# Hyena's transforms over odd frequencies, split into even and odd tokens, inside a two-layer mixer network

## The chip, the cores and the metric

The kernel runs on one core of one Trainium2 chip. The metric is device time in microseconds (us) of the whole network: the median of three runs before the change is 2637.45 us, from 2637.12 to 2638.57. A difference of about 0.2%, here 5 us, is the least that a comparison of two such kernels can tell from no change.

Engines have the names of the profile: PE is TensorE, PEld its weight loads, DVE is VectorE, ACT is ScalarE, POOL is GpSimd, and SP (SPq in rows) is the engine that issues the DMAs here.

## The reference, cut to what matters

Two layers work on 256 latent tokens and 256 context tokens of width 1024. A layer is a SwiGLU FFN, four token mixers on one normalised input (MLA, gated linear attention "GLA", GQA, and Hyena), merged by gates, and a second FFN. In the second layer the context's mixer output isn't needed. The change touches Hyena alone:

```python
def hyena_filters(L, w1, b1, w2, b2, w3):
    ...
    h = h * jnp.exp(-t[:, None] * deltas[None, :])[:, None, None, :]
    full = jnp.concatenate([h[:, :, 0], jnp.zeros(...), jnp.flip(h[1:, :, 1], axis=0)], axis=0)
    return jnp.fft.rfft(full.astype(jnp.float32), axis=0)

def fft_long_conv(u, filt_f, bias):
    L = u.shape[1]
    U = jnp.fft.rfft(u.astype(jnp.float32), n=2 * L, axis=1)
    y = jnp.fft.irfft(U * filt_f[None], n=2 * L, axis=1)[:, :L]
    return (y + u * bias).astype(u.dtype)

def hyena_mixer(p, hy):
    z = lax.conv_general_dilated(p, sconv_w[:, None, :], ...) + sconv_b
    x1, x2, v = jnp.split(z, 3, axis=-1)
    filt = hyena_filters(p.shape[1], w1, b1, w2, b2, w3)
    v = x1 * fft_long_conv(v, filt[:, 0], fbias[0])
    v = x2 * fft_long_conv(v, filt[:, 1], fbias[1])
    return v
```

Each of the 512 channels of a sequence of L = 256 tokens is convolved with a filter that reaches 255 tokens to both sides, then multiplied by a gate, twice ("orders", `od` 0 and 1 in the code).

## The kernel before

**Matmuls.** Every large product is done as three matmuls of the type fp32r: each operand is held as a rounded part ("h", a CAST on ACT) and a rest ("l", a subtraction on DVE), and `mm3` (L305) adds h·h, h·l and l·h into PSUM. `two` (L311) makes such a pair: `nc.scalar.copy` for h and `nc.vector.tensor_sub` for l. Weights come from DRAM by DMAs on SP into three buffers `wr` and are split in the same way into `wh` and `wl` (eight buffers each), 512 columns at a time, on ACT and DVE. While `self.share` is set, which is in the second layer's Hyena and GLA stage alone, the rest `wl` is made on POOL instead.

**Transforms as matmuls.** `tables` (L100) holds three matrices of 256 tokens by 256 frequencies (`dft`: cosines, negative sines, and the sines of the way back, with the Nyquist frequency in a row of their own). `dft(n)` (L1084) loads n of them and splits each into a pair.

**Filters.** `filters` (L1105) makes the spectra of both layers' filters once, in the first FFN, where its steps are fillers between the FFN's rows. For each layer and order it makes the filter in time (`h3`, tiles `hx`), forms sum and difference of its two directions on POOL (L1155, L1156), splits them (`hy`), and multiplies by the tables: for two halves m of the frequencies and for real and imaginary part e, six matmuls `sp` of 512 channels. Four more matmuls `nyq` with one column of weights give the Nyquist row. The spectra go to DRAM (`hs`, five tiles for each layer and order) from SBUF tiles `spx` and `spn` of the pool `t`, which has six buffers.

**Hyena.** `hyena` (L1189) runs for both sequences in the first layer (`nseq` = 2) and for the latent one in the second (`nseq` = 1). It projects and convolves over three tokens (`conv`, PSUM tile `dp`). For each order it transposes the current value to tokens (eight 128x128 transposes `zT` a sequence), splits it (`zth`, `ztl`), and for each sequence does 24 matmuls `Z` of 512 channels (two halves m, real and imaginary part), the complex product with the spectrum on DVE (L1241 to L1246), the split into `Y`, and 48 matmuls `yi` of 256 tokens, which have the channels as weights' columns, so that the result has channels on the partitions again. The gate `gx` is multiplied there (L1260, L1263).

**Order of the work.** A scheduler of the programming layer sets the order on each engine when the program is built, from priorities and from its own picture of when results are ready; each engine then works strictly in that order. `weave` (L1302) alternates between "chains", which have a raised priority, and a "fill". In the first layer the chain is `hyena`, the fill is `prep` (all other projections, PSUM tile `tm`). In the second layer the chains are `hyena` and `gla`, the fill is two `merge`s (PSUM tile `gate`). In `gla` (L951) the matmuls `AT` need the decayed keys `ab` (L1017), and the transposes `obT` the normalised output `z` (L1073), both from DVE. PSUM has two buffers each for the tags `S` (which `Z`, `sp`, `ada` and others use) and `T` (`zT`, `yi` and others).

Of the kernel before, what the change touches and what calls it, by code (L numbers as in the profile page):

```python
# [44 lines left out]
for _n, _w in (("kcos", 64), ("ksin", 64), ("spec", 2)):  # L45
    TAB[_n] = (_o, _w)
    _o += _w
# [18 lines left out]
          "end2": {"p": 11, "y": 4, "Yh": 4, "Yl": 4, "lv": 6, "lg": 4}}  # L66
SHARE = {"first": {"x": "v"},
         "ffn": {"x": "v"},
         "mix": {k: v for v, ks in (("v", "x hv mv lv"), ("p", "hp hH mp qp lp yh"), ("g", "hg mg qg lg yl"),
# [30 lines left out]
def tables():  # L100
# [17 lines left out]
    sp = np.full((P, 2), 2.0 / 512, np.float32)  # L118
    sp[0, 0] = 1.0 / 512
    put("spec", sp)  # L120
# [4 lines left out]
    T["ident"] = np.eye(P, dtype=np.float32)  # L125
    t = np.arange(L)
    ang = 2 * np.pi * ((t[:, None] * t[None, :]) % 512) / 512
    fre, fim = np.cos(ang), -np.sin(ang)
    ifim = fim.copy()
    fim[:, 0] = ifim[0, :] = (-1.0) ** t  # L130
    T["dft"] = np.stack([m.reshape(2, P, L).transpose(1, 0, 2) for m in (fre, fim, ifim)], 0).reshape(3, P, 512)
# [4 lines left out]
    T["feat"] = np.concatenate([tl[:, None], np.cos(fw), -np.sin(fw)], -1).T  # L136
    dl = np.abs(np.linspace(math.log(1e-2) / 1.5, math.log(1e-2) / 0.3, 512, dtype=np.float32))
    wf = np.exp(-tl[:, None] * dl[None, :]).astype(np.float32)
# [83 lines left out]
class Net:  # L222
# [150 lines left out]
    def load(self):  # L373
# [24 lines left out]
        self.hs = self.dram.tile([DEPTH, 2, 5, P, 512], F32, name="hs")  # L398
# [706 lines left out]
    def filters(self):  # L1105
# [25 lines left out]
        F = self.dft(2)  # L1131
# [4 lines left out]
        for l in range(DEPTH):  # L1136
            for od in range(2):
# [26 lines left out]
                sp = self.tab["spec"]  # L1164
                for m in range(2):
                    for e in range(2):
                        p = self.pss("sp")
                        for k in range(2):
                            c = slice(k * L + m * P, k * L + m * P + P)
                            self.mm3(p, (F[e][0][:, c], F[e][1][:, c]), ab[k][e], k == 0, k == 1)  # L1170
                        x = self.t("spx")
                        nc.scalar.activation(x, p, AF.Copy, scale=sp[:, m:m + 1])
                        if m == 0 and e == 1:
                            nc.gpsimd.memset(x[0:1], 0.0)
                        nc.sync.dma_start(out=self.hs[l, od, 2 * m + e], in_=x)
                        if m == 0 and e == 0:
                            pn = self.pst("nyq")
                            for k in range(2):
                                c = slice(k * L, k * L + 1)
                                for i, z in enumerate(ab[k][0]):  # L1180

                                    self.mm(pn[:1], F[1][0][:, c], z, k == 0 and i == 0, k == 1 and i == 1)
# [226 lines left out]
```

## Time and profile before

| | before |
|---|---|
| median of three runs | 2637.45 us |
| profiled execution | 2630.62 us |
| its span (first to last instruction) | 2628.8 us |
| mean granted TensorE clock | 0.989 |
| PE busy | 2536.3 us, 96% |
| DVE busy | 1663.5 us, 63% |
| ACT busy | 1088.0 us, 41% |
| POOL busy | 241.7 us, 9% |

The profile is of one execution. Its 2628.8 us of span lie in 2630.62 us of device time; the median of the runs without a profile is 6.83 us above that. A PE row's length runs from the start of a matmul to its modelled end and overlaps the next one, so the pace of a row of matmuls is read from start to start. The same goes for DVE, whose instructions overlap by some 0.08 us. Three stretches matter: about 60 to 225 us, where the filters are made within the first FFN; 475 to 700 us, the first layer's Hyena; and 2125 to 2325 us, the second layer's Hyena and GLA.

### The profile page before, as it was taken

To read this page: it belongs to the slowest core of one execution; us is meant where nothing else is said; L and a number is where in the kernel's file an instruction comes from. 1 tells how busy PE (TensorE), PEld (TensorE's weight loads), DVE (VectorE), ACT (ScalarE), POOL (GpSimd) and SP (SyncE) were. 2 spreads that over 40 slices of the span, in tenths; PEclk is the share of its full clock that TensorE was granted. 3 is DMA by queue.
4 is the path that set the end of the run, shared out by engine and by line. 5 is a ranking of instruction groups with operands and counts; after the bars stand their busy time and mean duration, and the time that the engine had idled before them with its cause. 6 is when DMAs were issued, how large, how long until landed. Compare 5 with 4: busy or idle time off the path is not lost. (4 is left out here: it accounts for less than half of the span.)

```text
span 2628.8 us, 37485 instructions
## 1 busy us (share of the span) xinstructions
PE 2536.3 (96%) x13952; PEld 2098.2 (80%) x13952; DVE 1663.5 (63%) x3326; ACT 1088.0 (41%) x2114; POOL 241.7 (9%) x232
## 2 busy tenths in 40 slices
PE   6999999999999999999999999999999988899998
PEld 4667888799976767786888878888888777798998
DVE  5556677655555868746744447767457666776665
ACT  4332323423455464433323233232345655355454
POOL 2120001200000000001000021000030045401000
PEclk9999999999999999999999999999999999899999
DMA  7436455433322323336543244545254334356554
GB/s 255 155 133 232 137 184 178 151 116 105 106 87 92 94 63 97 96 104 211 175 143 96 93 137 150 182 143 181 85 176 161 104 124 150 97 170 213 175 181 126
DMA packets 123901, 371.93 MB, mean 141 GB/s; under 512 B 14210, under 2 KB 19780, under 8 KB 123720
## 3 DMA queue, kind: packets, MB, share of 16 engines
q1 hardware_dynamic: 123720, 369.55, 43.5%
q8 instruction: 110, 1.80, 0.3%
q14 instruction: 71, 0.58, 0.1%
HBM read 348.00 MB, written 21.50 MB: 141 GB/s over the span
## 5 line engine op out<-in xcount | busy, mean ns | idle before, releaser
L313 ACT CAST wh<-wr 128x512 fp32r<-128x512 f32 (+1 forms) x926 | 564.2, 613 | 1090.7 <-PE gu L303 395.5
L314 DVE TENSOR_TENSOR wl<-wr,wh 128x512 fp32r<-128x512 f32 (+1 forms) x854 | 578.2, 683 | 449.9 <-ACT wh L313 439.0
L303 PE MATMUL gu<-ul,wh 128*128 128x512 f32 (+1 forms) x1408 | 514.2, 366 | 2.8 <-DVE ul L544 2.7
L303 PE MATMUL gu<-uh,wh 128*128 128x512 f32 (+1 forms) x1408 | 511.8, 365 | 2.5 <-ACT uh L538 2.3
L303 PE MATMUL gu<-uh,wl 128*128 128x512 f32 (+1 forms) x1408 | 511.1, 364 | 1.3 <-DVE wl L314 1.3
L303 PE MATMUL dn<-hh,wh 128*128 128x512 f32 (+1 forms) x1408 | 391.8, 365 | 0.0
L303 PEld LDWEIGHTS gu<-ul,wh 128*128 128x128 f32 x1408 | 266.2, 189 | 58.4 <-DVE ul L544 8.0
L303 PEld LDWEIGHTS gu<-uh,wh 128*128 128x128 f32 x1408 | 266.6, 190 | 51.2 <-ACT uh L538 7.0
L303 PEld LDWEIGHTS gu<-uh,wl 128*128 128x128 f32 x1408 | 266.2, 189 | 43.8 <-issue 2.0
L303 PEld LDWEIGHTS dn<-hh,wh 128*128 128x128 f32 x1408 | 255.1, 190 | 41.7
L303 PE MATMUL dn<-hh,wl 128*128 128x512 f32 (+1 forms) x704 | 256.8, 365 | 0.0
L504 POOL TENSOR_TENSOR nacc<-nacc,sq 128x512 f32<-128x512 f32 (+1 forms) x39 | 46.0, 1178 | 1773.0 <-ACT sq L502 1765.6
L303 PE MATMUL gate<-uh,wh 128*128 128x256 f32 (+1 forms) x768 | 200.9, 326 | 0.0
L466 DVE SCALAR_TENSOR_TENSOR aj<-aw,crow 128x1024 bf16<-128x1024 f32 x160 | 194.0, 1225 | 3.0 <-DMA crow<-cb 3.0
L303 PE MATMUL gate<-uh,wl 128*128 128x512 f32 (+1 forms) x512 | 176.0, 344 | 0.3 <-POOL wl L314 0.3
L303 PEld LDWEIGHTS dn<-hh,wl 128*128 128x128 f32 x704 | 133.9, 190 | 20.8
L303 PE MATMUL tm<-wh,uh 128*128 128x256 f32 x576 | 140.0, 288 | 1.6 <-ACT uh L538 1.0
L303 PEld LDWEIGHTS gate<-uh,wh 128*128 128x128 f32 x768 | 130.7, 194 | 11.6 <-issue 2.3
L303 PE MATMUL tm<-wl,uh 128*128 128x256 f32 x432 | 124.0, 287 | 0.0
L314 POOL TENSOR_TENSOR wl<-wr,wh 128x512 fp32r<-128x512 f32 x72 | 100.8, 1412 | 245.4 <-ACT wh L313 225.7
L303 PE MATMUL tm<-wh,ul 128*128 128x256 f32 x416 | 107.8, 286 | 0.0
L303 PEld LDWEIGHTS gate<-uh,wl 128*128 128x128 f32 x512 | 98.7, 193 | 11.2 <-issue 1.7
(390 smaller groups left out, 4023.1 us busy)
## 6 DMA issues: line engine op xcount, KB each, us to landing
wr<-in_gu SPq DMA_DIRECT2D x176, 512.0 KB, 3.5
aw<-in_adat SPq DMA_DIRECT2D x80, 512.0 KB, 3.6
wr<-in_dn SPq DMA_DIRECT2D x64, 512.0 KB, 3.8
wr<-in_w_gate SPq DMA_DIRECT2D x64, 512.0 KB, 3.5
aw<-in_ada SPq DMA_DIRECT2D x48, 512.0 KB, 5.3
wr<-in_w_tm SPq DMA_DIRECT2D x36, 512.0 KB, 3.5
wr<-in_w_br SPq DMA_DIRECT2D x32, 512.0 KB, 3.5
wr<-in_dn SPq DMA_DIRECT2D x32, 384.0 KB, 3.2
```

Of the source, the lines that this page charges most:

```text
L303: self.nc.tensor.matmul(out, l, r, start=start, stop=stop)
L313: self.nc.scalar.copy(h, src)
L314: (eng or self.nc.vector).tensor_sub(l, src, h)
L466: nc.vector.scalar_tensor_tensor(out=x, in0=w, scalar=1.0, in1=self.crow[s], op0=ALU.mult, op1=ALU.mult, accum_out=o[:, s:s + 1])
L504: (nc.vector if first and k % 2 else nc.gpsimd).tensor_add(acc[:, :n], acc[:, :n], sq[:, :n])
```

## The change

The transforms are taken at odd frequencies, at the angles 2π(2f+1)t/1024, f from 0 to 255, instead of 2πft/512. Frequency 255 − f has, but for signs, the same values as f: with the tokens split by parity, the even tokens' sum and the odd tokens' sum of the first 128 frequencies give f as their sum and 255 − f as their difference. So one table of 128 points, in four blocks of 128x128 (cosine and negative sine, even and odd tokens), serves in place of three of 256 by 256, and one more holds the blocks transposed for the way back. There is no Nyquist row.

- `half` (new) does one block: three matmuls of 512 channels, or six where it adds a second block.
- In `filters` each part e takes two halves (12 matmuls `sp` for a layer and order in place of 24, and no `nyq`), and DVE makes sum and difference of them from PSUM (two instructions for each e), ACT a scaled copy. Four stores in place of six.
- In `hyena` a sequence of one order takes 12 matmuls `Z`; ACT copies one half, DVE makes sum and difference (`za`, `zb`); the complex products are ten DVE instructions and two on POOL; four more on DVE combine f with 255 − f before the way back; four pairs `Yh`, `Yl`; 12 matmuls `yi` of 512 channels whose weights are the table's blocks. The result has tokens on the partitions, all even or all odd ones.
- So for order 0 the gates are transposed to tokens (`yT`, eight transposes of every second token) and multiplied there, and the product is split at once for order 1 (`nz`), which needs no transpose of its own. For order 1 the result is copied by ACT, transposed back (eight `yT`), and multiplied by every second token of the gate, in eight DVE instructions of 128x128.
- Four spectrum tiles `H` are loaded in place of five, two tables in place of three. In the second layer's stage the pools are eight in place of eleven `p`, three in place of four `Yl`, and four new `za`.

```diff
-          "end2": {"p": 11, "y": 4, "Yh": 4, "Yl": 4, "lv": 6, "lg": 4}}
+          "end2": {"p": 8, "y": 4, "za": 4, "Yh": 4, "Yl": 3, "lv": 6, "lg": 4}}
...
-         "mix": {k: v for v, ks in (("v", "x hv mv lv"), ("p", "hp hH mp qp lp yh"), ("g", "hg mg qg lg yl"),
+         "mix": {k: v for v, ks in (("v", "x hv mv lv"), ("p", "hp hH mp qp lp yh"), ("g", "hg za mg qg lg yl"),
...
     t = np.arange(L)
-    ang = 2 * np.pi * ((t[:, None] * t[None, :]) % 512) / 512
-    fre, fim = np.cos(ang), -np.sin(ang)
-    ifim = fim.copy()
-    fim[:, 0] = ifim[0, :] = (-1.0) ** t
-    T["dft"] = np.stack([m.reshape(2, P, L).transpose(1, 0, 2) for m in (fre, fim, ifim)], 0).reshape(3, P, 512)
+    ang = 2 * np.pi * ((t[:, None] * (2 * np.arange(P)[None, :] + 1)) % 1024) / 1024
+    fwd = [f(ang[e::2]) * g for f, g in ((np.cos, 1.0), (np.sin, -1.0)) for e in range(2)]
+    T["dft"] = np.stack([np.concatenate(fwd, 1), np.concatenate([m.T for m in fwd], 1)])
+    par = np.concatenate([t[0::2], t[1::2]])
...
-        self.hs = self.dram.tile([DEPTH, 2, 5, P, 512], F32, name="hs")
+        self.hs = self.dram.tile([DEPTH, 2, 4, P, 512], F32, name="hs")
...
-        F = self.dft(2)
+        F = self.dft(1)[0]
...
-                sp = self.tab["spec"]
-                for m in range(2):
...
-                            nc.sync.dma_start(out=self.hs[l, od, 4, 0:1], in_=xn[0:1])
+                for e in range(2):
+                    p = [self.half(F, 2 * e + k, ab[k][e], "sp") for k in range(2)]
+                    x, y, z = (self.t("spx") for _ in range(3))
+                    nc.scalar.activation(x, p[0], AF.Copy, scale=2.0 / 512)
+                    nc.vector.scalar_tensor_tensor(out=y, in0=p[1], scalar=2.0 / 512, in1=x, op0=ALU.mult, op1=ALU.add)
+                    nc.vector.scalar_tensor_tensor(out=z, in0=p[1], scalar=(2 * e - 1) * 2.0 / 512, in1=x,
+                                                   op0=ALU.mult, op1=ALU.subtract if e else ALU.add)
+                    nc.sync.dma_start(out=self.hs[l, od, 2 * e], in_=y)
+                    nc.sync.dma_start(out=self.hs[l, od, 2 * e + 1], in_=z)
                 yield
+    def half(self, F, q, x, name, y=None, r=0):
+        p = self.pss(name)
+        for q, x, last in ((q, x, y is None), (r, y, True)):
+            if x is not None:
+                c = slice(q * P, q * P + P)
+                self.mm3(p, (F[0][:, c], F[1][:, c]), x, y is None or not last, last)
+        return p
     def hyena(self, l, u, nseq, out):
         nc, A = self.nc, self.A
@@ -1206,64 +1199,95 @@
         for i in range(4):
             conv(8 + i, src[i])
             yield
-        F = self.dft(3)
+        F, G = self.dft(2)
+        def parity(x, s, e):
+            return x[:, s * L + e:s * L + L:2]
+        zt = []
+        for i in range(2 * nseq):
+            T = self.pst("zT")
+            for c in range(4):
+                self.tr(T[:, c * P:c * P + P], parity(src[c], i // 2, i % 2))
+            h, lo = self.tl("o", "zth", 512, F32R), self.tl("o", "ztl", 512, F32R)
+            self.two(h, lo, T)
+            zt.append((h, lo))
+        yield
         for od in range(2):
-            zt = []
-            for t in range(2 * nseq):
...
-            H = [self.ld(self.tl("hH", "H"), self.hs[l, od, i]) for i in range(5)]
+            H = [self.ld(self.tl("hH", "H"), self.hs[l, od, i]) for i in range(4)]
             gx = self.packed("hg" if od else "hv", "hx", n, 4)
             for i in range(4):
                 conv(4 * od + i, gx[i])
                 if i % 2:
                     yield
-            if od == 0:
-                dst = self.packed("hv", "z1", n, 4)
-            else:
+            if od:
                 dst = [self.pair("o", "od", n) for _ in range(4)]
+            nz = []
             for s in range(nseq):
+                z = []
+                for e in range(2):
+                    p = [self.half(F, 2 * e + k, zt[2 * s + k], "Z") for k in range(2)]
+                    x, y = self.tl("za", "za"), self.tl("za", "zb")
+                    nc.scalar.copy(y, p[0])
+                    nc.vector.tensor_add(x, y, p[1])
+                    if e:
+                        nc.vector.tensor_sub(y, p[1], y)
+                    else:
+                        nc.vector.tensor_sub(y, y, p[1])
+                    z += [x, y]
+                yield
+                a, b, c, d = z
+                q = []
+                for x, y, hx, hy in ((a, c, H[0], H[2]), (b, d, H[1], H[3])):
+                    v, w = self.t("yv"), self.t("yw")
+                    nc.gpsimd.tensor_mul(v, y, hy)
+                    nc.vector.tensor_mul(w, x, hx)
+                    nc.vector.tensor_mul(x, x, hy)
+                    nc.vector.tensor_mul(y, y, hx)
+                    nc.vector.tensor_sub(w, w, v)
+                    nc.vector.tensor_add(x, x, y)
+                    q.append(w)
+                nc.vector.tensor_sub(d, a, b)
+                nc.vector.tensor_add(a, a, b)
+                nc.vector.tensor_add(c, q[0], q[1])
+                nc.vector.tensor_sub(b, q[0], q[1])
                 Y = []
-                for m in range(2):
-                    pz = []
...
-                        self.mm3(p[:, :L], (Y[q][0][:, cc], Y[q][1][:, cc]), (f[0][:, fc], f[1][:, fc]), q == 0, q == 3)
+                for x in (c, d, b, a):
+                    Y.append((self.tl("Yh", "Yh", 512, F32R), self.tl("Yl", "Yl", 512, F32R)))
+                    self.two(*Y[-1], x)
+                yield
+                T = []
+                for e in range(2):
+                    p = self.half(G, e, Y[2 * e], "yi", Y[2 * e + 1], 2 + e)
+                    T.append(self.pst("yT"))
+                    x = self.t("yx")
+                    for c in range(4):
+                        if od == 0:
+                            self.tr(T[e][:, c * P:c * P + P], parity(gx[c], s, e))
                     if od == 0:
-                        nc.vector.tensor_mul(dst[c][:, cs], p[:, :L], gx[c][:, cs])
+                        nc.scalar.copy(x, T[e])
+                        nc.vector.tensor_mul(x, p, x)
+                        h, lo = self.tl("o", "zth", 512, F32R), self.tl("o", "ztl", 512, F32R)
+                        self.two(h, lo, x)
+                        nz.append((h, lo))
                     else:
-                        x = self.t("od")
-                        nc.vector.tensor_mul(x[:, :L], p[:, :L], gx[c][:, cs])
-                        self.two(dst[c][0][:, cs], dst[c][1][:, cs], x[:, :L])
+                        nc.scalar.copy(x, p)
+                        for c in range(4):
+                            self.tr(T[e][:, c * P:c * P + P], x[:, c * P:c * P + P])
+                if od:
+                    cs = slice(s * L, s * L + L)
+                    for c in range(4):
+                        if c % 2 == 0:
+                            x = self.t("od")
+                        xc = x[:, c % 2 * L:c % 2 * L + L]
+                        for e in range(2):
+                            nc.vector.tensor_mul(xc[:, e::2], T[e][:, c * P:c * P + P], parity(gx[c], s, e))
+                        self.two(dst[c][0][:, cs], dst[c][1][:, cs], xc)
                 yield
-            src = dst
+            zt = nz
         out.extend(dst)
```

PE, first layer, first sequence of order 0. `Z` are the transforms, `tm` the fill's projections, `yi` the way back. Before (the line of dots stands for the tm rows up to 37 in all):

```order
L303 MATMUL Z<-ztl,dfth 128x512
L303 MATMUL tm<-wl,uh 128x256
L303 MATMUL Z<-zth,dftl 128x512
L303 MATMUL tm<-wh,ul 128x256
...
L303 MATMUL tm<-wh,ul 128x256
L303 MATMUL yi<-dfth,Y 128x256
L303 MATMUL tm<-wh,uh 128x256
L303 MATMUL yi<-dftl,Y 128x256
```

Now (the dots stand for the tm rows up to 84 in all):

```order
L301 MATMUL Z<-zth,dfth 128x512
L301 MATMUL Z<-ztl,dfth 128x512
L301 MATMUL Z<-zth,dftl 128x512
L301 MATMUL tm<-wh,ul 128x256
...
L301 MATMUL tm<-wl,uh 128x256
L301 MATMUL yi<-Yh,dfth 128x512
L301 MATMUL tm<-wh,ul 128x256
L348 MATMUL yT<-ident,hx 128x128
```

The scheduler puts 84 matmuls of the fill between the last `Z` and the first `yi` where it put 37. At the first layer's three other places of this kind there are now 82 `tm`, 73 `tm`, and 21 `tm` with 24 `bk` of 512 columns. The transposes `yT` stand one by one between other matmuls. In the second layer more than 200 `gate` and `dp` rows, and GLA's, stand between the last `Z` and the first `yi` of each order.

DVE at the same place, from the first use of the last `Z` on. `wl` is the fill's weights. Before:

```order
L1243 TENSOR_TENSOR yb<-Z,H 128x512
L1244 TENSOR_TENSOR yd<-Z,H 128x512
L1245 TENSOR_TENSOR ya<-ya,yb 128x512
L1246 TENSOR_TENSOR yc<-yc,yd 128x512
L314 TENSOR_TENSOR Y<-ya,Y 128x512
L314 TENSOR_TENSOR Y<-yc,Y 128x512
```

Now (the dots stand for a copy `vr` of the fill, the sum of `za`, and for `zb` the same five products and sums):

```order
L1234 TENSOR_TENSOR za<-zb,Z 128x512
L1236 TENSOR_TENSOR zb<-Z,zb 128x512
L1246 TENSOR_TENSOR yw<-za,H 128x512
L1248 TENSOR_TENSOR za<-za,H 128x512
L1247 TENSOR_TENSOR za<-za,H 128x512
L1249 TENSOR_TENSOR yw<-yw,yv 128x512
...
L1255 TENSOR_TENSOR za<-yw 128x512
L1253 TENSOR_TENSOR zb<-za,zb 128x512
L312 TENSOR_TENSOR wl<-wr,wh 128x512
L1254 TENSOR_TENSOR za<-za,zb 128x512
L312 TENSOR_TENSOR Yl<-za,Yh 128x512
```

Three instructions led from there to the value that is split first (L1245), on values of both parts; now there are fourteen with the copy, up to the row L1255, after which ACT makes the first `Yh`.

SP, the stores of the third spectrum. Before:

```order
L322 DMA wr<-in_dn 128x1024 x5
L1175 DMA hs<-spx 128x512
L1183 DMA hs<-spx 127x512
L1186 DMA hs<-spn 1x512
L1175 DMA hs<-spx 128x512 x2
L291 DMA fb<-in_hfb 1x512
L1175 DMA hs<-spx 128x512
```

Now:

```order
L320 DMA wr<-in_dn 128x1024 x5
L1169 DMA hs<-spx 128x512
L1170 DMA hs<-spx 128x512
L289 DMA fb<-in_hfb 1x512
L1169 DMA hs<-spx 128x512
L1170 DMA hs<-spx 128x512
```

The store of one row, `hs<-spn`, is gone, and with it the store of the other 127.

## Rows read from the trace of the kernel before

**Rows 1.** The page: busy us, share of the span, and instructions of each engine.
```profile
PE 2536.3 (96%) x13952; PEld 2098.2 (80%) x13952; DVE 1663.5 (63%) x3326; ACT 1088.0 (41%) x2114; POOL 241.7 (9%) x232
```

**Rows 2.** Windows: length, then busy us (instructions) of PE, PEld, DVE, ACT, POOL.
```profile
475.00:700.00 225.00, 224.07 (x1414) 200.53 (x1411) 128.12 (x219) 78.87 (x147) 10.17 (x17) 1.00 0.34 114
2125.00:2325.00 200.00, 173.01 (x1263) 158.26 (x1262) 147.49 (x286) 99.82 (x194) 90.57 (x65) 0.95 0.40 127
60.00:225.00 165.00, 152.00 (x646) 115.15 (x645) 84.97 (x137) 58.90 (x99) 25.26 (x20) 0.96 0.50 170
```

**Rows 3.** Timeline of PE, filters: start, length, instruction.
```profile
191.85 1.09 PE L303 MATMUL nyq<-hy,dfth 128*1 128x512 f32 x4
192.78 0.62 PE L303 MATMUL sp<-hy,dfth 128*128 128x512 f32 x2
...
196.89 0.61 PE L303 MATMUL dn<-hh,wh 128*128 128x512 f32 x2
```

**Rows 4.** Timeline of PE, second layer's last way back.
```profile
2314.20 0.53 PE L303 MATMUL yi<-dfth,Y 128*128 128x256 f32 x3
2314.56 0.28 PE L303 MATMUL yi<-dftl,Y 128*128 128x256 f32 x1
```

**Rows 5.** Timeline of PE, transposes among other matmuls.
```profile
502.48 0.82 PE L350 MATMUL zT<-ident,hv 128*128 128x128 f32 x6
503.06 0.36 PE L303 MATMUL tm<-wh,ul 128*128 128x256 f32 x1
```

**Rows 6.** Groups of PE: shape, count, busy us and mean ns, idle before.
```profile
L303 PE MATMUL yi<-dfth,Y 128*128 128x256 f32 x192 | 48.1, 287 | 3.2 <-DVE Y L314 3.0
L303 PE MATMUL sp<-hy,dfth 128*128 128x512 f32 x64 | 20.6, 400 | 2.3 <-ACT spx L1172 2.0 <-DVE hy L314 0.2
L303 PE MATMUL Z<-zth,dfth 128*128 128x512 f32 x48 | 19.2, 404 | 0.0
L350 PE MATMUL zT<-ident,z 128*128 128x128 f32 x24 | 5.1, 279 | 0.0
L303 PE MATMUL nyq<-hy,dfth 128*1 128x512 f32 x16 | 4.4, 395 | 0.0
```

**Rows 7.** Timeline of DVE: full, half and quarter width.
```profile
545.23 0.68 DVE L1243 TENSOR_TENSOR yb<-Z,H 128x512 f32<-128x512 f32 x1
545.83 0.68 DVE L1244 TENSOR_TENSOR yd<-Z,H 128x512 f32<-128x512 f32 x1
...
2261.85 0.61 DVE L1073 SCALAR_TENSOR_TENSOR z<-Og,l_rs,sg 128x128 f32<-128x128 f32 x2
...
2316.07 0.75 DVE L314 TENSOR_TENSOR od<-od 128x256 fp32r<-128x256 f32 x2
```

**Rows 8.** Timeline of ACT, a cast of the first layer.
```profile
555.55 0.62 ACT L313 CAST Y<-ya 128x512 fp32r<-128x512 f32 x1 [5.41 <-DVE ya L1245]
```

**Rows 9.** Timeline of POOL, filters.
```profile
186.85 1.29 POOL L1155 TENSOR_TENSOR hdif<-hx 128x512 f32<-128x512 f32 x1
188.22 1.63 POOL L1156 TENSOR_TENSOR hx<-hx 128x512 f32<-128x512 f32 x1
```

**Rows 10.** Timeline of DVE beside the second of these.
```profile
188.62 1.78 DVE L314 TENSOR_TENSOR hy<-hdif,hy 128x512 fp32r<-128x512 f32 x1
```

**Rows 11.** Waits of PE, 2125 to 2325: us in total, times, longest.
```profile
PE AT L303 <- DVE ab L1017: 8.0, 2, 5.2
PE obT L350 <- DVE z L1073: 6.3, 3, 3.2
```

**Rows 12.** Waits, 160 to 195.
```profile
DVE hx L1149 <- DMA hs<-spx: 5.0, 1, 5.0
PE h L303 <- DVE hx L1149: 4.9, 1, 4.9
```

**Rows 13.** SP's queue, the store of one row.
```profile
166.96 5.07 SPq L1186 DMA_DIRECT2D hs<-spn  x1
```

**Rows 14.** DMA issues: size, median us to landing.
```profile
hs<-spx SPq DMA_DIRECT2D x16, 256.0 KB, 6.9
```

More of the change, by code (lines that the diff above doesn't have):

```diff
@@ L44 @@
 _o = 0
-for _n, _w in (("kcos", 64), ("ksin", 64), ("spec", 2)):
+for _n, _w in (("kcos", 64), ("ksin", 64)):
     TAB[_n] = (_o, _w)
@@ L117, in tables @@
     T["scan"] = sc
-    sp = np.full((P, 2), 2.0 / 512, np.float32)
-    sp[0, 0] = 1.0 / 512
-    put("spec", sp)
     T["tab"] = tab
@@ L135, in tables @@
     fw = w[:, None] * f[None, :]
-    T["feat"] = np.concatenate([tl[:, None], np.cos(fw), -np.sin(fw)], -1).T
+    T["feat"] = np.concatenate([tl[:, None], np.cos(fw), -np.sin(fw)], -1).T[:, par]
     dl = np.abs(np.linspace(math.log(1e-2) / 1.5, math.log(1e-2) / 0.3, 512, dtype=np.float32))
-    wf = np.exp(-tl[:, None] * dl[None, :]).astype(np.float32)
+    wf = np.exp(-tl[:, None] * dl[None, :]).astype(np.float32)[par]
     T["win"] = wf.reshape(2, P, 512)
@@ L1163, in filters @@
                 yield
-                sp = self.tab["spec"]
-                for m in range(2):
[L1166 to L1182, printed above, removed]
-                            nc.sync.dma_start(out=self.hs[l, od, 4, 1:], in_=x[1:])
-                            xn = self.t("spn")
-                            nc.vector.tensor_scalar_mul(xn[0:1], pn[0:1], 1.0 / 512)
-                            nc.sync.dma_start(out=self.hs[l, od, 4, 0:1], in_=xn[0:1])
@@ L1208, in hyena @@
             yield
-        F = self.dft(3)
-        for od in range(2):
-            zt = []
-            for t in range(2 * nseq):
-                T = self.pst("zT")
-                for c in range(4):
-                    self.tr(T[:, c * P:c * P + P], src[c][:, t * P:t * P + P])
-                h, lo = self.tl("o", "zth", 512, F32R), self.tl("o", "ztl", 512, F32R)
-                self.two(h, lo, T)
-                zt.append((h, lo))
-            yield
-            H = [self.ld(self.tl("hH", "H"), self.hs[l, od, i]) for i in range(5)]
+        F, G = self.dft(2)
[10 more added lines that the diff above has]
+        yield
+        for od in range(2):
+            H = [self.ld(self.tl("hH", "H"), self.hs[l, od, i]) for i in range(4)]
             gx = self.packed("hg" if od else "hv", "hx", n, 4)
```

24 lines of the change are left out of this document (removed).

## The prediction, made before the result was known

> **What bounds the kernel now.** I read the page's busy times first: PE is busy for 2536.3 of 2628.8 us, DVE for 1663.5 [rows 1]. A PE that is busy need not be one that is fed, so the windows come next. In the first layer's Hyena PE is busy for 224.07 of 225 us, with DVE at 128.12; in the filters for 152.00 of 165; in the second layer's Hyena and GLA for 173.01 of 200, with DVE at 147.49 and POOL at 90.57, 45% against 9% of the whole span [rows 1, 2]. So in the first two stretches what is taken off PE comes off the time, as long as no wait replaces it. In the third PE already waits for DVE, for 8.0 us before `AT` and 6.3 us before `obT`, both steps of GLA [rows 11], and there a saving of PE work is worth less than its size.
>
> **PE's price list.** From start to start, 18 matmuls `sp` of 512 columns take 196.89 − 192.78 = 4.11 us, 0.228 each; four `nyq` take 192.78 − 191.85 = 0.93, 0.23 each, as much as full ones [rows 3]. Three matmuls `yi` of 256 columns take 0.36, 0.12 each [rows 4]. Six transposes take 0.58, 0.097 each, and the matmul behind them is 0.36 long where its kind is 0.28, so a change of kind costs some 0.08 more [rows 5].
>
> **What the change does to PE.** Counts of before are in [rows 6]; `mm3` makes two matmuls with the table's rounded part for one with its rest, so 64 `sp` rows mean 96 matmuls, 192 `yi` rows 288, and `Z` has three rows of 48, 144.
>
> - Filters (four spectra): 96 `sp` become 48, and 16 `nyq` go: 64 × 0.228 = 14.6 us less.
> - Hyena, for each order and sequence (six in all, four in the first layer): `Z` 24 → 12, 2.74 us less; `yi` from 48 × 0.12 = 5.76 to 12 × 0.228 = 2.74, 3.02 us less; transposes 48 in all → 24 `zT` and 48 `yT`, four more on average, and they stand singly: 0.39 for these plus eight changes of kind at 0.08, 1.0 us more. Net 4.7 us each.
> - First layer 4 × 4.7 = 18.9 us, second 2 × 4.7 = 9.5 us. With the filters, 43 us of PE work less.
>
> Every second token as a transpose's input is new: no row shows such a read on PE. At best it costs nothing; if each of the 48 that read so (24 `zT`, 24 `yT` of order 0) took double, 4.7 us. I take 1, near the plain transpose.
>
> **What it does to DVE and POOL.** DVE's full-width instructions start 0.60 us apart (545.83 − 545.23); two half-width ones take 0.75, 0.38 each, two quarter ones 0.61, 0.31 each [rows 7]. For order 0 a sequence goes from 18 full and 4 half (12.3 us) to 26 full (15.6); for order 1 from 16 full and 8 half (12.6) to 22 full, 4 half and 8 quarter (17.2). That is 7.9 us more for both orders: 16 us in the first layer, on 128 of 225, and 8 us in the second, on 147 of 200. ACT gains four instructions of 0.62 [rows 8] for each order and sequence and has room in all three stretches [rows 2]. POOL gets two products of 1.3 to 1.6 us each [rows 9].
>
> These products don't run free beside DVE. While POOL's `hx` ran from 188.22 for 1.63 us, DVE's `hy<-hdif,hy` took 1.78 us in place of 0.69 [rows 9, 10]: 1.1 us for one meeting. The Trainium skill, SBUF — State Buffer, "Who interferes with whom", says that a VectorE instruction with two SBUF inputs and a GpSimd one that reads SBUF exclude each other for the whole instruction. The pair of rows agrees. By that rule all twelve products would be added to DVE's time in full, and the rival on POOL below is what that does here.
>
> **First layer: does the fill cover the longer chain?** The engines keep the order they are given. After the last `Z` of the first place PE has 84 `tm` before `yi`, 84 × 0.12 = 10.1 us. DVE has fourteen instructions until the first sum is ready, 8.4 us, one meeting with POOL, 1.1, and ACT's cast, 0.6: 10.1 us. At the others I count thirteen DVE instructions, 9.5 us, against 82 × 0.12 = 9.8, 73 × 0.12 = 8.8, and 21 × 0.12 + 24 × 0.228 = 8.0 us. So PE waits for about 0, 0, 0.7 and 1.5 us before the first `yi`, and about as much again where the later `Y` come one DVE instruction at a time: I take 4 us in all. The ends are 0, if the order was made with the right durations, and 16, if each chain stops PE for four us more, about the 22 full instructions of a chain (13.2 us) and its cast and meetings (2.8) less the longer covers. Behind a waiting `yi` on PE stand only `tm` rows, whose weights' splits would be late by as much.
>
> **Second layer.** PE's 9.5 us come off a stretch where GLA's steps wait for DVE. DVE gets 8 us of work and POOL four products that can each hold it for 1.1, 12.6 us in all, among instructions of GLA; the fill is `gate` rows, whose weights are split on POOL behind these products. DVE's share would go from 74% to some 160 of 190 us, 84%. I take half of the 12.6 as new waits, 6 us; the ends are 0 (Hyena's rows stand where DVE idles) and 18 (all of it, and POOL's splits late by four products of 1.3). Net here 9.5 − 6 = 3.5.
>
> **Filters.** The two more DVE instructions for each part are covered by the FFN, whose stretch has DVE at 85 of 165. SP loses the 5.07 us at the store of one row [rows 13]. It held back the stores of `spx` behind it, and their buffers: DVE waited 5.0 us for such a store to land, and PE 4.9 for DVE [rows 12]. That one can go. But there are now six tiles `spx` for six buffers, four of which wait for stores that take 6.9 us to land [rows 14], and the next step is reached earlier by the removed matmuls: the wait can come back in any of three steps. I take nothing for it, with ends of −5 (the wait is gone) and +6 (three times 2 us).
>
> **The sum.** 43 us less on PE, 1 for the reads of every second token, 4 and 6 for waits: 32 us less. The profiled execution's own 2630.62 us become 2598.6; the median of the runs was 6.83 above it, so I forecast 2605 us, 1.2% faster. All ends on the good side (no waits, no cost of reads, −5) give 48 us less, 2589; all on the bad side (4.7, 16, 18, 6) cost 45, and nothing is left.
>
> **The rivals.**
>
> - *The saving passes through nearly whole.* Covers hold, Hyena's DVE rows fall where DVE idles in the second layer, and the filters' wait goes: 43 + 5 − 3 = 45 us, 2592. For it: the first layer's PE waits less than 1 us in 225 before. Against it: the first place's 10.1 against 10.1.
> - *POOL's products hold the chains.* All twelve meet DVE on the path, 1.3 us each (15.6), and in the second layer the `gate` weights' splits on POOL come late by 4 × 1.3 more, with the 4 and 3 us of DVE's own length: 28 us back, 43 − 28 = 15 us less, 2622. For it: [rows 9, 10], and POOL is 45% busy in the second layer. Against it: in the first layer the first product of each place runs while DVE reads PSUM, and POOL is idle there.
> - *The chain becomes the bound, and the kernel is slower.* The place is the way from `Z` to `yi`, in all six. If DVE takes the chain's 22 instructions in one piece, 13.2 us, plus 2.8 for cast and meetings, the splits of the fill's weights stand behind it and the cover ends with them: PE idles. It decides from 43 / 6 = 7.2 us of new wait for each place. With no cover at all it is 16 − 6 us of the old chain's length, 10 each, 60 in all: 17 us slower, 2654. Against it: eight buffers of split weights hold 4096 columns, four weight tiles, and in the second layer the order leaves more than 200 `gate` and `dp` rows in between.
> - *It doesn't do what it says for the path:* another engine's pace sets the FFN stage, so the filters' 14.6 us are returned as waits for weights: 32 − 15 = 17 us less, 2620.
>
> **How the numbers follow.** The forecast has 0.52, the full saving 0.18, POOL's products 0.13, the filters' return 0.07, the slower case 0.06; 0.04 remains for returns that come out within 5 us, about 0.2%, which is what a measurement can tell from no change. The range is 2588 to 2622: it takes in the second, third and last rival, leaves out the slower case and the remainder, and the forecast's own case lies between 2597 and 2613. Faster 0.90, same 0.04, slower 0.06.
>
> **What would show it.** In the profile after: `Z` 72, `sp` 48 and `yi` 72 matmuls, no `nyq`; PE's busy time down by about 35 to 43 us. Where the first layer's Hyena runs, PE stays above 97% busy, with waits of `yi` for `Yh` or `Yl` of 2 to 8 us in all. In the second, waits of PE for DVE grow by 3 to 10 us, and the stretch is shorter by less than 8. Single DVE rows of `yw` or `za` near 1.7 us beside `yv` on POOL. No SP row of 5 us at a store of `hs`. I am wrong if the first layer's stretch isn't shorter by 10 us or more, if transposes of every second token are spaced by 0.2 us, or if the filters' stretch isn't shorter.

## The result, and the profile after

The changed kernel takes 2606.49 us (median of four runs, 2601.85 to 2606.54; before beside it 2637.28). Its ratio to before is 0.9887, 95% interval 0.9873 to 0.9901: 30 us faster. The profiled execution took 2601.85 us with a span of 2600.1, at a mean granted clock of 0.986.

The page's busy line, columns as in [rows 1]; then three windows, columns as in [rows 2], with the granted clock, the DMA engines' busy share and GB/s at the end. The first two are moved by 28.15 and 35 us, so that they hold the same part of the program.

```profile
PE 2497.5 (96%) x13624; PEld 2058.8 (79%) x13624; DVE 1696.6 (65%) x3377; ACT 1091.1 (42%) x2127; POOL 264.9 (10%) x240
```

```profile
446.85:671.85 225.00, 217.01 (x1302) 190.31 (x1299) 153.13 (x269) 92.54 (x175) 22.27 (x25) 0.98 0.34 113
2090.00:2290.00 200.00, 163.73 (x1139) 145.28 (x1138) 150.68 (x285) 98.75 (x193) 102.88 (x69) 0.91 0.36 115
60.00:225.00 165.00, 160.90 (x717) 126.13 (x716) 114.64 (x194) 61.91 (x107) 23.28 (x16) 1.00 0.57 198
```

PE's busy time fell by 38.8 us. It is fed better in the filters (160.90 of 165 in place of 152.00) and worse in both Hyenas (217.01 in place of 224.07, 163.73 in place of 173.01). The groups of PE have the forecast counts, columns as in [rows 6]:

```profile
L301 PE MATMUL sp<-hy,dfth 128*128 128x512 f32 x32 | 11.3, 423 | 3.7 <-ACT spx L1165 1.7 <-ACT hy L311 1.0 <-DVE hy L312 0.9
L301 PE MATMUL yi<-Yh,dfth 128*128 128x512 f32 x24 | 10.6, 443 | 6.5 <-ACT Yh L311 6.5
L301 PE MATMUL Z<-zth,dfth 128*128 128x512 f32 x24 | 10.4, 441 | 1.6 <-ACT zth L311 1.4 <-ACT zb L1233 0.2
L348 PE MATMUL yT<-ident,hx 128*128 128x128 f32 x24 | 6.3, 294 | 2.0 <-DVE hx L1195 2.0
```

To see where the time went I cut each profile at four PE rows: the first `dp` (Hyena of the first layer begins), the first `wo` behind that layer's mixers, the first `lrT` of the second layer's Hyena and GLA, and the first `wo` behind these. Lengths in us:

| kernel | to first `dp` | layer 1, `dp` to `wo` | `wo` to `lrT` | layer 2, `lrT` to `wo` |
|---|---|---|---|---|
| before | 473.7 | 670.8 | 953.0 | 291.0 |
| after | 445.6 | 662.7 | 954.2 | 297.2 |
| before_one_store | 461.0 | 670.5 | 954.4 | 290.7 |
| before_new_filters | 444.2 | 670.1 | 956.6 | 291.0 |
| after_one_row_store | 469.3 | 659.4 | 954.8 | 298.5 |
| after_one_row_pool | 473.4 | 661.1 | 954.9 | 296.4 |
| after_products_dve | 450.0 | 655.3 | 952.4 | 298.0 |
| after_more_fill | 448.5 | 657.1 | 953.3 | 295.1 |
| after_dve_more_fill | 445.8 | 653.8 | 952.0 | 292.7 |
| after_dve_two_more_fill | 449.2 | 655.6 | 956.0 | 297.7 |
| after_l2_direct | 447.9 | 661.0 | 953.7 | 295.7 |
| after_l2_dve_as_before | 450.2 | 661.0 | 953.3 | 284.4 |
| after_l2_dead_dve_load | 447.1 | 663.8 | 956.5 | 290.2 |
| after_contiguous | 445.6 | 660.6 | 953.5 | 302.1 |

So the filters gave 28.1 us, the first layer 8.0, and the second took 6.2 back. The forecast was 14.6, 13.9 and 3.5. One profile stands for each kernel; where the code of a stretch is the same, its lengths differ by up to some 5 us (445.6 to 450.2 up to the first `dp`, 659.4 to 663.8 in layer 1, 952.0 to 956.6 from `wo` to `lrT`), so smaller differences in one cell say little. In layer 1 that spread is the granted clock: of the six kernels with the code of after there, the one at 659.4 has it in full throughout, the three near 661 have 3.4 us at half clock, after has 6.8 and the one at 663.8 has 10.2; half of that time is lost. That the second layer is longer rests on more than one cell: three kernels with its code of before show 290.7 to 291.0, three with that of after 296.4 to 298.5.

### The profile page after: what moved, and what is told of

It is laid out like the page before. It is cut to its first block, busy times and chain, and to the rows that moved or that the text cites. A ratio compares the mean times of both kernels' runs of the same rounds, so it can differ in the third digit from the quotient of the medians.

```text
span 2600.1 us, 36866 instructions
## 1 busy us (share of the span) xinstructions
PE 2497.5 (96%) x13624; PEld 2058.8 (79%) x13624; DVE 1696.6 (65%) x3377; ACT 1091.1 (42%) x2127; POOL 264.9 (10%) x240
## 5 line engine op out<-in xcount | busy, mean ns | idle before, releaser
L312 POOL TENSOR_TENSOR wl<-wr,wh 128x512 fp32r<-128x512 f32 x72 | 106.4, 1489 | 239.9 <-ACT wh L311 234.1
L642 DVE SCALAR_TENSOR_TENSOR x<-dn,gt,x 128x256 f32<-128x256 f32 x168 | 74.4, 478 | 54.6 <-PE dn L301 54.6
```

The costliest lines, as they stand in the source:

```text
L312: (eng or self.nc.vector).tensor_sub(l, src, h)
L642: self.nc.vector.scalar_tensor_tensor(out=self.x[m][:, c], in0=p[:, c], scalar=gt[:, m, s:s + 1], in1=self.x[m][:, c], op0=ALU.mult, op1=A ...
```

## The experiments

All ratios are to before, run beside the kernel.

**1. Filters: the stores or the matmuls?** `before_one_store`:

```diff
-nc.sync.dma_start(out=self.hs[l, od, 4, 1:], in_=x[1:])
+nc.sync.dma_start(out=self.hs[l, od, 4], in_=x)
-nc.sync.dma_start(out=self.hs[l, od, 4, 0:1], in_=xn[0:1])
```

> The kernel before, with the two stores of 127 rows and of one row of the odd spectrum replaced by one store of 128 rows (row 0 of the fifth spectrum tile is then the wrong value; matmuls nyq and their DVE row stay). Theory S: the one-row store, 5 us of SP's queue, made PE wait and fall to the half clock in the filters, and its removal is worth about as much again as the removed matmuls. Then the first dp of the first layer comes 8 to 14 us earlier than the 473.71 us of before, the PE wait for hx (5.05 us) and the half clock from 180 to 187 us are gone, and the kernel takes some 2627 us. Rival M: the matmuls alone made the filters shorter (a PE stage that waits less for weights behind them). Then the first dp stays within 3 us of 473.7 and the time within 3 us of before.

It took 2618.47 us, ratio 0.9939 (0.9927 to 0.9952), with the first `dp` 12.7 us earlier: theory S holds, and with more in the total than its estimate. The half clock that it expected to be gone is only shorter: 180.4 to 187.2 us before, 181.9 to 185.3 here. The window from 60 to 230 us, of before and of this kernel:

```profile
60.00:230.00 170.00, 157.00 (x668) 119.30 (x667) 89.97 (x149) 60.15 (x101) 25.26 (x20) 0.96 0.50 171
```

```profile
60.00:230.00 170.00, 165.41 (x731) 128.23 (x730) 102.13 (x171) 64.59 (x110) 25.25 (x20) 0.99 0.56 192
```

PE does 63 more matmuls in the same 170 us and the granted clock goes from 0.96 to 0.99. Before, PE waited 4.9 us there for `hx` [rows 12] and, by the view of waits, also for these; here 0.7 us are left of `ada` and nothing of the other two:

```profile
PE cbT L350 <- ACT cb L452: 3.1, 1, 3.1
PE ada L303 <- DMA aw<-in_ada: 2.8, 2, 2.6
```

**2. The new filters alone.** `before_new_filters` has `filters` and `half` of the changed kernel, and in Hyena:

```diff
-self.hs[l, od, i]) for i in range(5)]
+self.hs[l, od, min(i, 3)]) for i in range(5)]
```

> The kernel before with the filters of the changed kernel (48 matmuls sp, sums on DVE, four stores), Hyena as it was, which loads four spectrum tiles and the fourth again for the fifth (its output is then not the reference's). Forecast term: 64 matmuls x 0.228 = 14.6 us. If the 28.15 us that the first dp came earlier in the changed kernel belong to the filters alone, the first dp comes at 445 to 447 here, and the kernel takes 2609 us or, if the rest of the network returns nothing, the same 28 us less than before. If part of it came from Hyena's tables or the pools, the first dp comes later, near 459 (14.6 us less).

2607.87 us, ratio 0.9895 (0.9881 to 0.9910), first `dp` at 444.2. The filters alone bring all of the gain: after's 0.9887 lies inside this interval, so the whole change to Hyena is worth nothing that these runs can tell. What the new filters bring beyond the store is 461.0 − 444.2 = 16.8 us, beside a forecast of 14.6 for the matmuls; one profile can't tell the two numbers apart.

**3. The two stores put back, on SP and on POOL.** `after_one_row_store`, for e = 0; `after_one_row_pool` has `nc.gpsimd` in its last line:

```diff
-nc.sync.dma_start(out=self.hs[l, od, 2 * e], in_=y)
+nc.sync.dma_start(out=self.hs[l, od, 0, 1:], in_=y[1:])
+nc.sync.dma_start(out=self.hs[l, od, 0, 0:1], in_=y[0:1])
```

> The changed kernel with the first spectrum of each order stored as 127 rows and one row in place of one store of 128 (same values). Theory S: SP stops about 5 us at each of the four stores of one row, PE waits for hx or hy behind it, and the first dp comes 8 to 14 us later than the 445.56 us of the changed kernel; time about 2612 to 2620. Rival M: the store is hidden, first dp within 3 us of 445.6, time within 3 us of the changed kernel's.

2627.87 us, ratio 0.9972 (0.9961 to 0.9982), first `dp` 23.8 us later than in after: S again, and far beyond its estimate. PE's two longest waits there, 60 to 230 us, are the kinds that before has with 4.9 and 2.8:

```profile
PE h L301 <- DVE hx L1147: 9.1, 2, 6.8
PE ada L301 <- DMA aw<-in_ada: 6.3, 1, 6.3
```

SP's queue in this kernel, where L1170 stores 127 rows and L1171 one row:

```profile
166.66 0.24 SPq L1170 DMA_DIRECT2D hs<-spx  x1
166.96 4.84 SPq L1171 DMA_DIRECT2D hs<-spx  x1
171.89 0.34 SPq L1174 DMA_DIRECT2D hs<-spx  x1
```

> after_one_row_store with the store of one row issued by POOL in place of SP; the store of 127 rows and all others stay on SP. Theory H (what costs is that SP is held 4 to 7 us at each store of one row, with the other stores and the weights' loads behind it): SP has no such row, and the first dp comes at 445 to 451 in place of 469.3, the time near 2607. Rival W (the store itself lands late and its buffer spx with it): dp stays at 460 or later, with PE waiting for hx, and the time above 2618.

2630.15 us, 0.9976 (0.9965 to 0.9987), first `dp` at 473.4. Theory H fell and its rival W held: in the same window PE waits 10.2 us for `hx`. SP's queue now, with the store of one row on POOL:

```profile
164.29 0.24 SPq L1170 DMA_DIRECT2D hs<-spx  x1
165.49 4.06 SPq L1174 DMA_DIRECT2D hs<-spx  x1
169.72 0.25 SPq L289 DMA_DIRECT2D fb<-in_hfb  x1
```

The hold stayed, and sits at whatever stands behind the store of 127 rows. What that store does is in the view of the DMA engines. Before, two stretches, 170 to 173 and 176 to 182 us (packets and the rate; then the queue's share of 16 engines):

```profile
DMA packets 41, 0.08 MB, mean 26 GB/s; under 512 B 3, under 2 KB 3, under 8 KB 41
...
q1 hardware_dynamic: 41, 0.08, 6.7%
```

```profile
DMA packets 85, 0.16 MB, mean 26 GB/s; under 512 B 8, under 2 KB 8, under 8 KB 85
...
q1 hardware_dynamic: 85, 0.16, 6.8%
```

Over these nine microseconds 0.24 MB go out at 26 GB/s and 6.8% of 16 engines, which is one engine at work. The store of 128 rows ahead had landed 4.4 us after its issue at 166.21. The three behind, issued from 172.08 to 173.96, make up the three microseconds between the two stretches (three times 256 KB in 0.81 MB):

```profile
DMA packets 437, 0.81 MB, mean 270 GB/s; under 512 B 42, under 2 KB 42, under 8 KB 437
```

What is left for the slow stretches is the store of 127 rows (254 KB), beside single rows of 2 KB. With 128 rows in its place, 163 to 169 us of `before_one_store`:

```profile
DMA packets 874, 1.85 MB, mean 308 GB/s; under 512 B 102, under 2 KB 102, under 8 KB 874
...
q1 hardware_dynamic: 874, 1.85, 81.1%
```

The Trainium skill, DMA: Bandwidth & Descriptors, "Why a DMA increments its semaphore by 16 and not by 1", says how many engines a DMA gets: the largest number up to 16 that divides the outermost sizes (other than 1) of both its sides, and it gives 127 partitions as a case of one engine. The trace agrees. A store of 127 rows by itself was not run; that it and not its pair costs the time follows from the bytes and from the run with the pair on POOL.

**4. Two ways to shorten or cover the chain from `Z` to `yi`.** `after_products_dve`, `after_more_fill`, and both:

```diff
-nc.gpsimd.tensor_mul(v, y, hy)
+nc.vector.tensor_mul(v, y, hy)
...
                     self.two(*Y[-1], x)
                 yield
+                yield
                 T = []
```

> The changed kernel with the two products yv of each place on DVE in place of POOL. Theory P (POOL's products share the port with DVE and lengthen the chain from Z to yi): the chain gets shorter by the meetings, 1.1 us each, against two DVE rows of 0.6 more; PE's waits of yi for Yh in the first layer (6.5 us) and the second layer's stretch from lrT to wo (297.2 us) get shorter, by 2 to 6 us in all. Rival D (DVE's length is what counts): twelve rows of 0.6 us more on DVE, 7 us, come back as waits, most of them in the second layer: 297.2 grows by 2 to 4 us, and the first layer's waits grow by up to 5 us.

> The changed kernel with the products yv on DVE (as in after_products_dve) and one more step of the fill between the splits Yh, Yl and the way back yi. Theory C (in the first layer the chain outlasts its cover): the waits of yi for Yh and Yl in the first layer, some 7 us in the changed kernel, go below 2, and dp to wo falls by a further 2 to 5 us below the 655.3 of after_products_dve; the time about 2596. Rival: the fill's weights are split on DVE behind the same chain, so PE then waits for wl instead, and nothing is gained (655 and 2600, within 2).

> The changed kernel with one more step of the fill before yi, products yv on POOL as they are: the fourth corner beside after, after_products_dve and after_dve_more_fill. If cover alone is what the first layer lacks, dp to wo is 654 to 656 as in after_dve_more_fill (653.8), and POOL's products cost nothing once the chain is covered; if the meetings on the port delay the fill's splits too, it stays 3 us or more above, near 658. Second layer: 292 to 295, as the cover gave 5 us with the products on DVE. Time about 2592 by the first, 2597 by the second.

> after_dve_more_fill with two more steps of the fill in place of one. The first layer's last place then has only 70 tm and four transposes before its last way back, the second layer's second place 68 gate and 96 dp in place of 138 gate and 48 dp. Theory: one step covers nearly all, so the first layer stays within 2 us of 653.8, the second of 292.7, and the time is within 3 us of 2590.7. Rival: the fill runs out and later work of the first layer has none, 3 to 8 us more.

| | ratio, 95% interval | us | PE's waits of `yi` in layer 1 |
|---|---|---|---|
| after | 0.9887 (0.9873 to 0.9901) | 2606.49 | 7.2 |
| products on DVE | 0.9865 (0.9851 to 0.9878) | 2599.80 | 3.7 |
| more fill | 0.9859 (0.9838 to 0.9879) | 2598.23 | 3.8 |
| both | 0.9832 (0.9815 to 0.9849) | 2590.70 | 1.6 |
| products on DVE, two more steps | 0.9880 (0.9860 to 0.9900) | 2604.88 | 2.7 |

Each edit alone halves the waits, and their medians are lower, though the intervals still touch that of after. Together they are faster beyond the intervals, by 0.56% or some 15 us: the version that beats both kernels. On the products theory P holds for the first layer, not for the second. The first is 7.4 us shorter than in after, of which 3.4 are what half clock costs after there; against `after_one_row_store`, which has the same first layer and the full clock (659.4), it is 4.1. On cover theory C holds as to the waits, its rival as to the further gain in the first layer (1.5 us); the second layer gained 5.3. A second step is worse by 14 us, more than its rival's 3 to 8, and not where it said: 5.0 us of the profile's loss lie in the second layer, 1.8 in the first and the rest in stretches whose code is the same. In `after_more_fill` the first layer came out between its two cases (at the first, 655.4, without the 1.7 us that half clock costs it), and the time at the second.

The first place of the changed kernel shows why cover was short. DVE, POOL, then PE:

```profile
519.47 1.34 DVE L1246 TENSOR_TENSOR yw<-za,H 128x512 f32<-128x512 f32 x1
520.74 1.78 DVE L1248 TENSOR_TENSOR za<-za,H 128x512 f32<-128x512 f32 x1
522.44 0.68 DVE L1247 TENSOR_TENSOR za<-za,H 128x512 f32<-128x512 f32 x1
```

```profile
518.97 1.30 POOL L1245 TENSOR_TENSOR yv<-za,H 128x512 f32<-128x512 f32 x1 [60.49 <-DVE za L1234]
520.22 1.74 POOL L1245 TENSOR_TENSOR yv<-zb,H 128x512 f32<-128x512 f32 x1
```

```profile
527.82 0.28 PE L301 MATMUL tm<-wl,uh 128*128 128x256 f32 x1
529.24 0.50 PE L301 MATMUL yi<-Yh,dfth 128*128 128x512 f32 x1 [1.14 <-ACT Yh L311]
```

Two DVE instructions, not one, are drawn out beside POOL's, by 0.66 and 1.10 us over the plain 0.68. At the other three places of layer 1 the same two take 1.34, 1.33 and 1.19, and 1.78, 1.77 and 1.78. The rule of the Trainium skill that the prediction weighed, SBUF — State Buffer, "Who interferes with whom", agrees with both: each ends some 0.54 us behind the end of POOL's product, as if most of it had run only then. The two longest of these waits are

```profile
615.28 0.50 PE L301 MATMUL yi<-Yh,dfth 128*128 128x512 f32 x1 [1.85 <-ACT Yh L311]
638.01 0.50 PE L301 MATMUL yi<-Yh,dfth 128*128 128x512 f32 x1 [2.72 <-ACT Yh L311]
```

and 0.5 and 1.7 us behind their ends the granted clock falls. Three windows of after, the first two in layer 1, with the clock in the third column from the end:

```profile
615.80:619.20 3.40, 3.40 (x14) 3.21 (x15) 3.40 (x6) 1.57 (x3) 0.00 (x0) 0.50 0.42 152
639.70:643.10 3.40, 3.40 (x10) 2.62 (x9) 3.40 (x7) 1.14 (x2) 0.00 (x0) 0.50 0.87 230
2192.70:2202.90 10.20, 5.17 (x25) 4.68 (x26) 10.17 (x15) 3.67 (x8) 5.80 (x5) 0.50 0.36 129
```

At 0.50, the 1.2 GHz level, half of the time in which PE is busy is lost. In layer 1 that is 3.4 us, and `after_dve_more_fill` has no such stretch there. Nor need the clock fall: `after_one_row_store` has the same two waits in layer 1, 1.84 and 2.67 us, and the full clock throughout:

```profile
469.32:1128.71 659.39, 644.41 (x3491) 507.99 (x3491) 455.87 (x973) 315.35 (x671) 23.60 (x27) 1.00 0.31 99
```

**5. Second layer: what gives PE's saving back?** `after_l2_direct` runs Hyena's code of before there, with odd-frequency tables:

```diff
-self.weave([self.hyena(l, u, nseq, od), self.gla(l, nq, ob)], merges())
+self.weave([self.hyena1(l, u, nseq, od), self.gla(l, nq, ob)], merges())
...
+H += [self.ld(self.tl("hH", "H"), self.hs[l, od, i]) for i in (m, m + 2)]
```

> The changed kernel whose second layer makes the same odd-frequency transforms without the split by parity, with four 256x256 tables in Hyena's code of before (24 matmuls Z, 48 of 256 columns yi, spectra read as they are stored; same result); first layer and filters as changed. Theory L2 (in the second layer the split loses more in waits than it takes off PE): the stretch from lrT to the first wo goes back from 297.2 us to about 291, the kernel to about 2600. Rival R (the 297.2 comes from something else, as the pools or the order of the first layer): it stays near 297 or, with 9.5 us more of PE work, goes to 305.

`after_l2_dve_as_before`, its core, for each k of the second layer; `after_l2_dead_dve_load` adds the last two lines behind the splits:

```diff
+x, y = [self.half(F, 2 * e + k, zt[k], "Z") for e in range(2)]
+nc.vector.tensor_mul(w, x, hx)
+nc.vector.tensor_mul(za, x, hy)
+nc.vector.tensor_mul(v, y, hy)
+nc.vector.tensor_mul(zb, y, hx)
+nc.vector.tensor_sub(w, w, v)
+nc.vector.tensor_add(za, za, zb)
+q += [w, za]
...
+for k in range(6):
+    nc.vector.tensor_add(v, q[1], q[3])
```

> The changed kernel whose second layer leaves out ACT's copy, the sums za and zb, POOL's products and the four sums of f with 255 - f (its output is then not the reference's): DVE does the same twelve products and sums and four splits an order as before the change, on PSUM, and PE has the changed, smaller work. Theory D (DVE's added rows and the longer chain give PE's saving back): the stretch from lrT to wo falls from 297.2 by 8 to 15 us, to 282 to 289, below before's 291. Rival O (order, buffers, transposes, half clock): it stays above 293.

> As after_l2_dve_as_before (second layer without ACT's copy, the sums and POOL's products; its output is not the reference's), with six DVE additions of full width an order put behind the splits whose result nobody reads: DVE then has as many rows as in the changed kernel (22 an order), but the chain from Z to yi stays short. Theory Load (the amount of DVE work decides in the second layer): the stretch from lrT to wo goes from 284.4 back by 5 to 9 us, to 289 to 293. Theory Chain (the length of the way from Z to yi decides): it stays within 2 us of 284.4, and the added load is absorbed where DVE idles.

The stretch from `lrT` to `wo` in windows of before, after, `after_l2_dve_as_before` and `after_l2_dead_dve_load`:

```profile
2097.48:2388.48 291.00, 262.76 (x1962) 241.59 (x1961) 207.17 (x397) 152.42 (x305) 99.25 (x71) 0.96 0.45 141
```

```profile
2062.47:2359.66 297.19, 258.19 (x1875) 233.11 (x1873) 216.73 (x410) 154.85 (x312) 111.58 (x75) 0.94 0.42 136
```

```profile
2064.57:2348.96 284.39, 255.26 (x1874) 232.21 (x1873) 211.94 (x398) 153.56 (x308) 102.53 (x71) 0.95 0.44 142
```

```profile
2067.35:2357.54 290.19, 258.25 (x1875) 235.11 (x1873) 215.13 (x410) 153.21 (x308) 102.19 (x71) 0.94 0.44 139
```

With DVE's work as before and PE's as after, the stretch is 6.6 us shorter than before's: theory D holds, and PE's saving is there to be had. That kernel took 2594.98 us (0.9853, 0.9828 to 0.9879). With the dead load it took 2597.38 (0.9855, 0.9834 to 0.9877): in the profile 5.8 us of the 12.8 come back, as Load said, but the medians can't tell the two kernels apart. How the rest divides between the longer chain and POOL's products stays open. The direct form took 2604.81 (0.9889, 0.9870 to 0.9909): it brought back less than a third of the way to before's 291, within what one profile varies by, and nothing in time. So theory L2 isn't borne out, and its rival R stays: with the pools of before and as many PE and DVE rows, the direct form is still some 4.7 us above before's 291, PE's waits for `obT` there are 9.5 us in place of 6.3, and no run shows why. Against the direct form, the split by parity costs the second layer 1.5 us, no more than the profiles vary by: its smaller PE work gives 295.7 − 284.4 = 11.3, its added DVE, ACT and POOL rows take 12.8 back.

PE's waits in the second stretch of after that before doesn't have (of the wait for `wl` it has 0.3):

```profile
PE AT L301 <- issue: 4.3, 1, 4.3
PE gate L301 <- DVE y L1316: 3.3, 1, 3.3
...
PE gate L301 <- POOL wl L312: 2.8, 1, 2.8
PE yT L348 <- DVE hx L1195: 2.0, 1, 2.0
PE Z L301 <- DVE ztl L312: 1.9, 1, 1.9
```

They are not those of one chain. They stand at the fill (`gate`), at GLA (`AT`, where the profile shows no releaser), and on both ends of Hyena; in three of the five DVE is late, in one POOL.

**6. Every second token.** `after_contiguous`:

```diff
-self.tr(T[:, c * P:c * P + P], parity(src[c], i // 2, i % 2))
+self.tr(T[:, c * P:c * P + P], src[c][:, i * P:i * P + P])
```

and the same for order 0's `yT`.

> The changed kernel with zT and order 0's yT reading 128 tokens side by side in place of every second token (the tokens are then in the wrong order, its output not the reference's); counts and the last multiply are unchanged. My forecast priced the reads of every second token at 1 us of PE in all, with 4.7 as the upper end. Their weight loads take 195 to 208 ns in the trace against 137 to 140 for contiguous ones. If that lies on PE's path, 48 x 0.06 = 3 us come off, two thirds in the first layer; if the loads are covered by the matmul before them, less than 1 us, below what the comparison can tell.

2606.52 us, 0.9889 (0.9869 to 0.9909): the same as after. The weight loads are shorter, but PE doesn't wait for them: less the half clock, layer 1 is 658.9 us long here and 659.3 in after. Two rows of PEld, of after and of this kernel:

```profile
529.58 0.20 PEld L348 LDWEIGHTS yT<-ident,hx 128*128 128x128 f32 x1
```

```profile
529.48 0.14 PEld L348 LDWEIGHTS yT<-ident,hx 128*128 128x128 f32 x1
```

Its second layer shows 302.1 us, with a granted clock of 0.91 in it: PE is busy 7.4 us longer there than in after (265.57 against 258.19) with the same matmuls, so how long that stretch is depends on the clock too.

## Why the prediction was right in sum and wrong in its terms

**Right: the PE work.** 64 × 0.228 = 14.6 us in the filters, measured 16.8 between two kernels with 128-row stores, where single profiles vary by some 5. In the first layer, PE's busy time from `dp` to `wo` falls from 662.47 us to 643.46 in `after_dve_more_fill`, where cover is good and the clock full: 19.0 against a forecast of 18.9 − 1. The reads of every second token cost nothing that can be seen; six such transposes start 0.105 us apart (0.63 from 474.36 on), against 0.097 before.

**Wrong: the filters' stores.** "I take nothing for it" was the step that failed most: it measured −12.7 us in `before_one_store`, outside its ends of −5 and +6. The prediction read SP's row of 5.07 us [rows 13] as a cost of the one-row store and counted one wait [rows 12]. The cause is the store ahead of it, whose own row on SP is short (0.24 us in experiment 3), and which leaves one DMA engine writing 254 KB: the buffer and the DMAs behind it are late, and the granted clock in the window is 0.96 where it could be 0.99.

**Too small: the waits in the first layer, "I take 4 us in all".** They are 7.2, inside the range given, because both of POOL's products meet DVE at each of the four places and I counted one meeting: the other adds 0.5 to 0.7 us, some 2.5 in all. What the half clock behind the waits costs, 3.4 us, stood in no term. 18.9 − 7.2 − 3.4 = 8.3 gives what was measured, 8.0. By the mark set beforehand, 10 us or more off this stretch, the step was wrong, though narrowly: the six kernels with this first layer are 7.0 to 11.4 us shorter than before, by how long they run at half clock. The other sign set there failed as well: PE is busy for 96.4% of the window, not above 97%.

**Wrong in sign: the second layer, 3.5 us less.** It is 6.2 us more. All of PE's waits in the stretch together grew from 27.7 to 38.6 us, 10.9 in place of 6. PE's busy time fell by only 4.6 us (262.76 to 258.19) in place of 9.5, as the granted clock fell from 0.96 to 0.94, which no term held. 10.9 − 4.6 = 6.3 is what was measured. Part of it came with the direct form too, so the cause stays partly open. (The forecast's 12.6 for DVE is 8 + 4 × 1.1 = 12.4; nothing hangs on it.) Of the rivals, the one on POOL's products has a part in the first layer: it priced them there at 8 × 1.3 = 10.4 us, and moving them to DVE gave 7.4, or 4.1 without the half clock. In the second layer that move changed nothing.

The two errors, 13.5 us too little in the filters and 15.6 too much in Hyena, cancelled. A forecast that lands within 2 us has not thereby shown its steps.

## What to carry to other kernels

Look at the outermost size of every store and load: 127 rows went out on one DMA engine here, at a small part of the rate that stores of 128 rows reached. Work taken off PE pays only as far as the chain that replaces it is covered, and where a second engine is at 73%, as DVE is in the second layer, that chain is felt as many small waits, at times with half-clock time behind them. Before giving two halves of a product to DVE and POOL, count both as one engine's work, as the 1.34 and 1.78 us rows show.

## What the hardware showed that was not expected

- SP was held 3.6 to 6.8 us at the DMA behind each store of 127 rows, whichever DMA that was, in three kernels, and the data went out at 26 GB/s where it could be watched alone.
- Of the gain of a change to the transforms, about half came from how a spectrum was stored: 16 us by the ratio (0.9939) of 30.
- fp32 weight loads of a transpose with every second element took 0.20 us in place of 0.14, hidden behind the matmul before them.
- Small waits can cost more than their length: in the second layer 10.9 us of new waits came with a granted clock of 0.94 in place of 0.96, and half of PE's saving was lost. But the same waits in the first layer came with anything from 0 to 10.2 us at half clock.
